# Attention row sums in a hybrid decoder layer: the diagonal pieces added on GpSimd in place of matmuls with a column of ones

## The chip, the cores and the metric

One core of one Trainium2 chip runs the whole layer in one launch. The metric is the device time in microseconds of an execution; the time before is the median of three runs. The profile shows one execution in full: TensorE matmuls (PE), its weight loads (PEld), VectorE (DVE), ScalarE (ACT), GpSimd (POOL), SyncE (SP, which issues the DMAs here) and the DMA queues.

## The reference, cut to what matters

16 learned meta tokens stand ahead of 2048 tokens (L = 2064, D = 1024). After a layer norm, one projection gives queries, keys, values, forget logits and gates for 16 heads of 64 columns, and the input of a causal pooling mixer. The attention is a causal softmax with a forget bias:

```python
s = jnp.einsum('bqhd,bkhd->bhqk', q_blk, k).astype(jnp.float32) * scale
s = s + jnp.transpose(c_blk, (0, 2, 1))[..., :, None] - c_k[:, :, None, :]
mask = key_pos[None, :] <= q_pos[:, None]
s = jnp.where(mask[None, None], s, -jnp.inf)
p = jax.nn.softmax(s, axis=-1).astype(v.dtype)
return jnp.einsum('bhqk,bkhd->bqhd', p, v)
```

Both mixers are gated, joined, projected with `w_out`, added to the scaled input and normalized again. All of it is float32. The change touches how the denominator of the softmax, the sum of `p` over the keys, is made.

## The kernel before, in words

**Stages.** The projections run first (to about 1360 us of the span), then the attention (`phase_b`, to about 2252), in which matmuls of the output projection are strewn between as filler, then the rest of the output projection and the last layer norm (`phase_c`).

**Precision.** A float32 value is kept as a high part in the matmul's own format (float32r) and a low part, the rest: `ph` and `pl` are the high and the low part of exp of the scores, `th` and `tl` those of a sum.

**Attention.** The queries of a head are cut into four blocks j = 0..3 of 512 (64 blocks for 16 heads; the first 14 heads in turn, the last two interleaved). A block works through its keys in units (`units`, line 903): units i = 0..4j are one tile of 128 keys for all 512 queries; unit 4j+1 has 400 queries left of the diagonal; the last unit, 4j+2, packs three pieces of 272, 144 and 16 queries. The piece of 16 is the corner: its keys are the 16 that 128-key tiles leave over, kept in rows 112 to 127 of `vc`. Units i < 4j lie wholly below the diagonal. There are 576 units in all.

**What a unit issues.** `emit_s` (line 959): two score matmuls per piece into the PSUM tile `s` (four buffers), a mask matmul in bf16 on the diagonal; ACT's exp into `ph`, and exp again over `s`. `emit_pl` (line 996): DVE's `pl` = `s` − `ph`, which frees the buffer of `s`. `emit_pv` (line 1015), four units later (`LAG`): the matmuls with the values. A value tile has the 64 low columns, the 64 high columns and two columns of ones, so `xo` collects `ph` times both halves, and `yo` collects `pl` times the high half, with the sum of `pl` in the rows behind it.

**The row sums of `ph`** come in two ways. For units i < 4j, POOL adds pairs of `ph` tiles (`acc` for the first pair, `tu` for others, three buffers; lines 988 to 994), DVE adds `tu` to `acc` three units later (line 1000), and behind the last of these it splits `acc` into `th` and `tl` (lines 1001 to 1006). Two matmuls with `zo`, whose first 64 columns are zero and last two are one, then add both to `yo` in the block's last unit (lines 1037 to 1039). For the units on the diagonal, each piece has a matmul of its own with `zo` (line 1036). A block with j = 0 has only these. The corner's three matmuls contract over rows 96 to 127 (lines 1030 and 1041).

When a block ends, ACT copies `yo` (`c1`), DVE adds the high and low parts into `araw`, and the sum's row goes out by DMA; every second head, `chunk_end` (line 917) brings the reciprocal back by DMA and gates: two multiplies and a subtraction on POOL, a cast on DVE.

**Order.** Instructions of PE, DVE, ACT and POOL are chained by hand in the order in which the program is written (`in_order`, line 65), so each engine's queue is that order. The loop at line 1085 writes for each unit m: its scores, then filler matmuls by a weight (two for units left of the last two, one for those), `emit_pl(m)`, `emit_pv(m - LAG)`, loads, and in every second unit a round of delayed work (`service`: gating, weight splits).

Of the kernel before, what the change touches and what calls it, by code (L numbers as in the profile page):

```python
# [9 lines left out]
F32 = mybir.dt.float32  # L10
# [25 lines left out]
def f32(ap):  # L36
    return ap.bitcast(F32)
# [3 lines left out]
def kernel(  # L41
# [78 lines left out]

    # rows of a head: c high and low, k high, k low, q low, q high, -max high and low
    kqd = dtile("kqd", [H, 260, L], F32)
# [603 lines left out]
    def kv_set(pl, s):  # L726
# [4 lines left out]
        nc.gpsimd.memset(f32(ka[0:2, :]), 1.0)  # L731
        nc.gpsimd.memset(f32(vc[96:P]), 0.0)
        for v in (vt, vc):
# [51 lines left out]
    def prefetch(n, nv):  # L785
        """Loads at most one piece of keys and values ahead of head order, and queries two steps ahead."""
        k = 0
# [171 lines left out]
    def emit_s(m):  # L959
# [27 lines left out]
        late_pl[m] = (ps, ph, pl, off)  # L987
        if i < 4 * j and i % 2:
            tag = "acc" if i == 1 else "tu"
            tu = bp.tile([P, 512], F32, tag=tag, name=tag, bufs=2 if i == 1 else 3)  # L990
            if i == 1:
                accs[n] = tu
            nc.gpsimd.tensor_tensor(out=tu, in0=f32(units_state[m - 1][0]), in1=f32(ph), op=ALU.add)
            units_tu[m] = tu

    def emit_pl(m):
        n, i, u, nu = seq[m]
        h, j = seqn[n]
        if 6 <= i and i % 2 == 0:
            nc.vector.tensor_tensor(out=accs[n], in0=accs[n], in1=units_tu.pop(m - 3), op=ALU.add)  # L1000
            if i == 4 * j + 2:
                th = bp.tile([P, 512], F32R, tag="th", name="th")
                tl = bp.tile([P, 512], F32R, tag="tl", name="tl")
                nc.vector.tensor_copy(out=th, in_=accs[n])
                nc.vector.tensor_tensor(out=tl, in0=accs[n], in1=f32(th), op=ALU.subtract)
                accs[n] = (th, tl)
        ps, ph, pl, off = late_pl.pop(m)
        nc.vector.tensor_tensor(
            out=pl[:, :off], in0=ps[:, :off], in1=f32(ph[:, :off]), op=ALU.subtract
        )  # L1010
# [4 lines left out]
    def emit_pv(m):  # L1015
# [9 lines left out]
        np_ = len(places)  # L1025
        full = i < 4 * j
        for idx, (kt, q0, w, off) in enumerate(places):
            first = i == 0 and idx == 0
            sl = slice(off, off + w)
            rows, v = (slice(96, P), vc[:, j]) if w == NM else (slice(0, P), vt[:, kt])  # L1030
            mm(
                xo[:, q0:512], v[rows, 0:P], ph[rows, sl],
                start=first, stop=last_u and idx == np_ - 1,
            )
            if not full:
                mm(yo[0 : DH + 2, q0:512], zo[rows], ph[rows, sl], start=first, stop=False)
        if last_u and j:
            for t in accs.pop(n):
                mm(yo[0 : DH + 2, :], zo, t, start=False, stop=False)
        for idx, (kt, q0, w, off) in enumerate(places):  # L1040
            rows, v = (slice(96, P), vc[:, j]) if w == NM else (slice(0, P), vt[:, kt])
            mm(
                yo[0 : DH + 2, q0:512], v[rows, DH:], pl[rows, off : off + w],
                start=full and i == 0 and idx == 0, stop=last_u and idx == np_ - 1,
            )
        if last_u:
            c1 = bp.tile([65, 512], F32, tag="c1", name="c1", bufs=2)
            nc.scalar.copy(out=c1, in_=yo[0:65, :])
# [36 lines left out]
    for m in range(nseq + LAG):  # L1085
# [11 lines left out]
        if m < nseq:  # L1097
            emit_pl(m)
        if m >= LAG:
            emit_pv(m - LAG)  # L1100
# [133 lines left out]
```

## Time and profile before

| | |
|---|---|
| Median of 3 runs | 2431.03 us (2428.52 to 2432.9) |
| Profiled execution, span from first to last instruction | 2432.5 us (mean granted clock 0.992; its device time is not listed apart from the span) |
| PE busy | 2366.8 us, 97%, 11706 matmuls |
| PEld busy | 1947.5 us, 80% |
| DVE busy | 1430.4 us, 59% |
| ACT busy | 960.6 us, 39% |
| POOL busy | 716.2 us, 29% |
| Matmuls of `ph` with `zo`, 512 wide | 64, mean 394 ns each |
| Matmuls `th` with `zo` | 48, mean 448 ns each |
| POOL pair sums `tu` / `acc` | 144 / 48, mean 1328 / 1301 ns |

A row of a group names the engine, the operation, out<-in by the program's names, the shape and the count. Matmuls record `out<-moving,stationary`, with rows*columns of the weights and then the moving tile; `128*66 128x512` is 66 columns of weights on 128 rows against 512 moving columns. Their records overlap, so the mean duration of one is longer than what it adds to the time. All instructions go through one helper, so all carry the line L86 and are told apart by their tiles.

### The profile page before, as it was taken

What the parts mean: (1) busy time and instruction counts of PE and PEld (TensorE: products, weight loads), DVE (VectorE), ACT (ScalarE), POOL (GpSimd) and SP (SyncE); (2) the same over time, 40 slices, a digit from 0 to 9 for tenths busy, and PEclk for the clock granted to TensorE, in tenths of its full rate; (3) what the DMA queues carried; (4) which work ended last, traced back from release to release, by engine and by line L of the source; (5) the groups of instructions that cost most, each with busy time, mean ns of one, the idle gap of its engine ahead of it and who ended that gap; (6) DMA issues with size and microseconds to landing.
All of it is one profiled execution on the core that took longest, in us unless ns stands there. A gap on an engine that the chain in (4) does not pass through costs nothing.

```text
span 2432.5 us, 32725 instructions
## 1 busy us (share of the span) xinstructions
PE 2366.8 (97%) x11706; PEld 1947.5 (80%) x11706; DVE 1430.4 (59%) x2116; ACT 960.6 (39%) x1813; POOL 716.2 (29%) x531
## 2 busy tenths in 40 slices
PE   6999999999999999999999899999999999999998
PEld 5778799898898988988887677777777777776787
DVE  6631145644655556545433578778778777777356
ACT  4431221211212222111111577777777777766000
POOL 4730021222223314230101134344353544444000
PEclk9999999999999999999999999999999999999999
DMA  7853222222222212222223657566566657555955
GB/s 254 262 162 92 61 85 61 96 63 78 88 62 88 81 60 88 68 92 75 75 81 111 174 159 210 153 189 181 168 187 179 199 168 215 161 164 158 286 187 164
DMA packets 317506, 333.59 MB, mean 137 GB/s; under 512 B 27744, under 2 KB 241072, under 8 KB 317312
## 3 DMA queue, kind: packets, MB, share of 16 engines
q1 hardware_dynamic: 317344, 331.51, 44.4%
q8 instruction: 92, 1.51, 0.3%
q14 instruction: 70, 0.57, 0.1%
HBM read 207.43 MB, written 124.00 MB: 136 GB/s over the span
## 4 chain that ended last, share of the span: by engine, by line
PE 91%; DVE 3%; DMA 2%; issue 1%; ACT 1%; POOL 0%; SPq 0%; DVEq 0%; ACTq 0%; POOLq 0%
PE d L86 59%; PE s L86 12%; PE yo L86 8%; PE mx L86 6%; PE xo L86 5%; DVE pl L86 1%; PE tr L86 1%; DMA xm<-xa 1%; DMA wu<-in_wut_dram 0%; SPq L86 0%; DVE acc L86 0%; DMA xt<-in_x_dram 0%; DVE s L86 0%; DMA wv<-in_wv_dram 0%; DMA kb<-kqd 0%
## 5 line engine op out<-in xcount | busy, mean ns | idle before, releaser
L86 PE MATMUL d<-hh,wh 128*128 128x412 f32 (+2 forms) x1472 | 561.4, 381 | 0.0
L86 PE MATMUL d<-hl,wh 128*128 128x412 f32 (+2 forms) x1472 | 538.6, 366 | 0.0
L86 PE MATMUL d<-hh,wl 128*128 128x412 f32 (+2 forms) x1472 | 538.4, 366 | 0.0
L86 DVE TENSOR_REDUCE mxs<-mx 128x1 f32<-128x912 f32 (+14 forms) x416 | 358.3, 865 | 279.1 <-PE mx L86 274.5
L86 DVE TENSOR_TENSOR pl<-s,ph 128x512 fp32r<-128x512 f32 (+2 forms) x576 | 376.3, 664 | 185.8 <-ACT s L86 179.6
L86 ACT ACTIVATE ph<-s 128x512 fp32r<-128x512 f32 (+2 forms) x576 | 335.0, 582 | 186.6 <-PE s L86 171.9
L86 PE MATMUL d<-wh,xm 128*128 128x512 f32 x1024 | 355.0, 403 | 4.6 <-DMA xm<-xa 3.8
L86 ACT ACTIVATE s<-s 128x512 f32<-128x512 f32 (+2 forms) x576 | 332.4, 577 | 0.0
L86 PEld LDWEIGHTS d<-hl,wh 128*128 128x128 f32 x1472 | 278.5, 189 | 23.1
L86 PEld LDWEIGHTS d<-hh,wl 128*128 128x128 f32 x1472 | 277.1, 188 | 23.4
L86 PEld LDWEIGHTS d<-hh,wh 128*128 128x128 f32 x1472 | 280.7, 191 | 18.2
L86 PE MATMUL s<-qa,ka 68*128 68x512 f32 (+4 forms) x704 | 265.2, 377 | 15.9 <-DVE pl L86 15.9
L86 POOL TENSOR_TENSOR wl<-wst,wh 128x1024 fp32r<-128x1024 f32 x40 | 96.2, 2405 | 576.4 <-ACT wh L86 576.3
L86 PE MATMUL s<-qb,kb 128*128 128x512 f32 (+4 forms) x704 | 253.0, 360 | 0.0
L86 POOL TENSOR_TENSOR tu<-ph 128x512 f32<-128x512 f32 x144 | 190.9, 1328 | 154.4 <-ACT ph L86 128.3
L86 PE MATMUL xo<-ph,vt 128*128 128x512 f32 (+3 forms) x640 | 233.0, 368 | 0.0
L86 PEld LDWEIGHTS d<-wh,xm 128*128 128x128 f32 x1024 | 193.5, 190 | 44.4 <-issue 3.3
L86 PE MATMUL yo<-pl,vt 128*66 128x512 f32 (+3 forms) x640 | 223.7, 366 | 0.9 <-ACT c L86 0.9
L86 PE MATMUL mx<-ka,qa 66*128 66x512 f32 (+5 forms) x704 | 199.4, 350 | 6.6 <-ACT qa L86 3.8
L86 PE MATMUL d<-wl,xm 128*128 128x512 f32 x512 | 205.6, 402 | 0.0
L86 PEld LDWEIGHTS s<-qa,ka 68*128 68x128 f32 x704 | 134.8, 191 | 71.6 <-DVE pl L86 27.4
L86 PEld LDWEIGHTS mx<-ka,qa 66*128 66x128 f32 x704 | 133.0, 190 | 23.8 <-ACT qa L86 5.2
(143 smaller groups left out, 3079.0 us busy)
## 6 DMA issues: line engine op xcount, KB each, us to landing
xm<-xp SPq DMA_DIRECT2D x32, 1024.0 KB
xm<-xa SPq DMA_DIRECT2D x20, 1024.0 KB
vd<-vs SPq DMA_DIRECT2D x32, 512.0 KB
vt<-vd SPq DMA_DIRECT2D x64, 256.0 KB
qb<-kqd SPq DMA_DIRECT2D x64, 256.0 KB
xa<-am SPq DMA_DIRECT2D x32, 512.0 KB
xp<-pm SPq DMA_DIRECT2D x32, 412.0 KB
kqd<-lo SPq DMA_DIRECT2D x64, 206.0 KB
```

The source lines that it names most:

```text
L86: return in_order(f(*a, **k))
```

## The change

The diagonal pieces' matmuls with `zo` go. In their place POOL adds the diagonal units into the same sums: unit 4j and unit 4j+1 into the last `tu`, DVE adds that to `acc` when the last unit's scores are issued, and POOL adds the last unit's three pieces to `acc`. A block with j = 0 starts `acc` from its first two units, with a copy for the 112 columns that the second does not have. `th` and `tl` are made for every block, two units after the last (`emit_sums`), and their matmuls come last in `yo`. The corner's matmuls contract over all 128 rows; for that `vc` is zeroed in all rows (the masked `ph` and `pl` are zero there).

```diff
@@ kv_set
-        nc.gpsimd.memset(f32(vc[96:P]), 0.0)
+        nc.gpsimd.memset(f32(vc), 0.0)
@@ emit_s
-        if i < 4 * j and i % 2:
-            tag = "acc" if i == 1 else "tu"
-            tu = bp.tile([P, 512], F32, tag=tag, name=tag, bufs=2 if i == 1 else 3)
-            if i == 1:
-                accs[n] = tu
-            nc.gpsimd.tensor_tensor(out=tu, in0=f32(units_state[m - 1][0]), in1=f32(ph), op=ALU.add)
-            units_tu[m] = tu
+        row_sums(m)
+
+    def pool_add(out, a, b):
+        nc.gpsimd.tensor_tensor(out=out, in0=a, in1=b, op=ALU.add)
+
+    def row_sums(m):
+
+        n, i, u, nu = seq[m]
+        h, j = seqn[n]
+        ph, _, places = units_state[m]
+        ph = f32(ph)
+        if i == 1:
+            accs[n] = bp.tile([P, 512], F32, tag="acc", name="acc", bufs=2)
+        if i < 4 * j:
+            if i % 2:
+                tu = accs[n]
+                if i > 1:
+                    tu = bp.tile([P, 512], F32, tag="tu", name="tu", bufs=3)
+                    units_tu[n, i] = tu
+                pool_add(tu, f32(units_state[m - 1][0]), ph)
+        elif i == 4 * j:
+            if j:
+                tu = units_tu[n, i - 1]
+                pool_add(tu, tu, ph)
+        elif i == 4 * j + 1:
+            (_, q0, w, off), = places
+            if j:
+                tu = units_tu[n, i - 2]
+                pool_add(tu[:, q0:], tu[:, q0:], ph[:, :w])
+            else:
+                first = f32(units_state[m - 1][0])
+                nc.gpsimd.tensor_copy(accs[n][:, :q0], first[:, :q0])
+                pool_add(accs[n][:, q0:], first[:, q0:], ph[:, :w])
+        else:
+            if j:
+                vec_add(n, i - 3)
+            for _, q0, w, off in places:
+                pool_add(accs[n][:, q0:], accs[n][:, q0:], ph[:, off : off + w])
+            sums_due.append((m + 2, n))
+
+    def vec_add(n, i):
+        nc.vector.tensor_tensor(out=accs[n], in0=accs[n], in1=units_tu.pop((n, i)), op=ALU.add)
+
+    sums_due = deque()
+
+    def emit_sums(m):
+        while sums_due and sums_due[0][0] <= m:
+            n = sums_due.popleft()[1]
+            th = bp.tile([P, 512], F32R, tag="th", name="th")
+            tl = bp.tile([P, 512], F32R, tag="tl", name="tl")
+            nc.vector.tensor_copy(out=th, in_=accs[n])
+            nc.vector.tensor_tensor(out=tl, in0=accs[n], in1=f32(th), op=ALU.subtract)
+            accs[n] = (th, tl)
@@ emit_pl
-        if 6 <= i and i % 2 == 0:
-            nc.vector.tensor_tensor(out=accs[n], in0=accs[n], in1=units_tu.pop(m - 3), op=ALU.add)
-            if i == 4 * j + 2:
-                th = bp.tile([P, 512], F32R, tag="th", name="th")
-                tl = bp.tile([P, 512], F32R, tag="tl", name="tl")
-                nc.vector.tensor_copy(out=th, in_=accs[n])
-                nc.vector.tensor_tensor(out=tl, in0=accs[n], in1=f32(th), op=ALU.subtract)
-                accs[n] = (th, tl)
+        if 6 <= i <= 4 * j and i % 2 == 0:
+            vec_add(n, i - 3)
@@ emit_pv
-        full = i < 4 * j
         for idx, (kt, q0, w, off) in enumerate(places):
             first = i == 0 and idx == 0
             sl = slice(off, off + w)
-            rows, v = (slice(96, P), vc[:, j]) if w == NM else (slice(0, P), vt[:, kt])
+            v = vc[:, j] if w == NM else vt[:, kt]
             mm(
-                xo[:, q0:512], v[rows, 0:P], ph[rows, sl],
+                xo[:, q0:512], v[:, 0:P], ph[:, sl],
                 start=first, stop=last_u and idx == np_ - 1,
             )
-            if not full:
-                mm(yo[0 : DH + 2, q0:512], zo[rows], ph[rows, sl], start=first, stop=False)
-        if last_u and j:
-            for t in accs.pop(n):
-                mm(yo[0 : DH + 2, :], zo, t, start=False, stop=False)
         for idx, (kt, q0, w, off) in enumerate(places):
-            rows, v = (slice(96, P), vc[:, j]) if w == NM else (slice(0, P), vt[:, kt])
+            v = vc[:, j] if w == NM else vt[:, kt]
             mm(
-                yo[0 : DH + 2, q0:512], v[rows, DH:], pl[rows, off : off + w],
-                start=full and i == 0 and idx == 0, stop=last_u and idx == np_ - 1,
+                yo[0 : DH + 2, q0:512], v[:, DH:], pl[:, off : off + w],
+                start=i == 0 and idx == 0, stop=False,
             )
         if last_u:
+            th, tl = accs.pop(n)
+            mm(yo[0 : DH + 2, :], zo, th, start=False, stop=False)
+            mm(yo[0 : DH + 2, :], zo, tl, start=False, stop=True)
             c1 = bp.tile([65, 512], F32, tag="c1", name="c1", bufs=2)
@@ loop over units
         if m < nseq:
             emit_pl(m)
+        emit_sums(m)
         if m >= LAG:
             emit_pv(m - LAG)
```

## The prediction

> **What bounds the kernel now.** I read the busy time by stage first, then the waits inside the longest stage that the diff touches, then single instructions. The stage runs from the last projection matmul to the last attention unit. Columns are the stretch, its length, busy time and instruction count of PE, PEld, DVE, ACT and POOL, the granted clock, and the DMA share and rate.
>
> ```profile
> 1360.00:2252.00 892.00, 874.90 (x4365) 661.16 (x4363) 690.79 (x1064) 651.52 (x1246) 376.52 (x286) 0.99 0.61 180
> 2252.00:2432.50 180.50, 167.88 (x720) 136.03 (x720) 94.03 (x139) 8.45 (x21) 4.26 (x3) 0.97 0.68 214
> ```
>
> The attention stage is 892 us of the span of 2432.5. PE is busy for 874.9 of them, DVE for 690.8 and POOL for 376.5. The waits of that stage say who holds PE up when something does (us in total, times, longest):
>
> ```profile
> PEld s L86 <- DVE pl L86: 27.4, 27, 3.0
> ...
> PE s L86 <- DVE pl L86: 15.9, 18, 2.6
> ```
>
> The two rows are one and the same wait seen from the weight load and from the matmul: the score matmul of a unit needs the PSUM bank that `pl`, four units earlier, has to give back. So some 27 us of the 892 are lost to DVE, and the rest is matmul after matmul. A matmul taken out shortens the stage by its slot, until DVE is late more often.
>
> **What a matmul costs here.** PE's records overlap, so a slot is the distance from one start to the next, not the duration in the second column. These rows are the last three units of one query block with j = 2:
>
> ```profile
> 1607.20 0.40 PE L86 MATMUL yo<-ph,zo 128*66 128x512 f32 x1
> 1607.43 0.39 PE L86 MATMUL yo<-pl,vt 128*66 128x512 f32 x1
> ...
> 1608.77 0.34 PE L86 MATMUL yo<-ph,zo 128*66 128x400 f32 x1
> 1608.94 0.35 PE L86 MATMUL yo<-pl,vt 128*66 128x400 f32 x1
> ...
> 1610.07 0.28 PE L86 MATMUL xo<-ph,vt 128*128 128x272 f32 x1
> 1610.19 0.29 PE L86 MATMUL yo<-ph,zo 128*66 128x272 f32 x1
> 1610.31 0.23 PE L86 MATMUL xo<-ph,vt 128*128 128x144 f32 x1
> 1610.38 0.23 PE L86 MATMUL yo<-ph,zo 128*66 128x144 f32 x1
> 1610.54 0.27 PE L86 MATMUL xo<-ph,vc 32*128 32x16 f32 x1
> 1610.67 0.20 PE L86 MATMUL yo<-ph,zo 32*66 32x16 f32 x1
> 1610.80 0.45 PE L86 MATMUL yo<-th,zo 128*66 128x512 f32 x1
> 1611.09 0.39 PE L86 MATMUL yo<-tl,zo 128*66 128x512 f32 x1
> 1611.32 0.35 PE L86 MATMUL yo<-pl,vt 128*66 128x272 f32 x2
> 1611.60 0.22 PE L86 MATMUL yo<-pl,vc 32*66 32x16 f32 x1
> 1611.75 0.50 PE L86 MATMUL s<-qa,ka 68*128 68x512 f32 x1
> 1612.09 0.40 PE L86 MATMUL s<-qb,kb 128*128 128x512 f32 x1
> ```
>
> The 512-wide matmul with the ones column has a slot of 0.23 us, the 400-wide one 0.17. The last unit, from its first matmul (1610.07) to the second score matmul behind it (1612.09), takes 2.02. In it every step into or out of the corner's 32 rows is long: 0.16 from the 144-wide matmul into the corner where the other 144-wide slot is 0.07; 0.13 and 0.13 inside; 0.29 for `th` and 0.34 for the next score matmul where a 512-wide one has 0.23. The next fence gives a 16-wide matmul on more rows, and the two ends of the last unit of a block with j = 0, which has no `th` and `tl` (1.56 us from 1636.74 to 1638.30):
>
> ```profile
> 1629.08 0.26 PE L86 MATMUL s<-qa,ka 68*128 68x16 f32 x1
> 1629.19 0.26 PE L86 MATMUL s<-qb,kb 128*128 128x16 f32 x1
> ...
> 1636.74 0.28 PE L86 MATMUL xo<-ph,vt 128*128 128x272 f32 x1
> ...
> 1638.30 0.39 PE L86 MATMUL s<-qb,kb 128*128 128x512 f32 x1
> ```
>
> A 16-wide score matmul, the next load being 128 columns wide, has a slot of 0.11. So sixteen columns are not what makes the corner slow; the change to 32 rows and back is the nearer reading. I take the long slots as gone once the corner uses all rows, and bound that from the other side below. The Trainium skill, page TensorEngine Tiling (Array Packing), section Key Properties, says that changing the tiling mode drains TensorE: by that rule the extra 0.09 to 0.11 at each switch goes with the 32 rows (67.5 us in the sum below), without it the gain would be 40. The trace agrees with the rule as far as it goes, since no corner on 128 rows has been run.
>
> **The change, part by part.** *Removed on PE.* Five matmuls with the ones column in each of the 64 query blocks. The new last unit I build from slots above: 272-wide 0.12; 144-wide before a 128-column load 0.11; corner 0.07 (there is no such row: it lies between 0.04 and the 0.13 of the old corner, and 0.07 is that of 144 columns before a 66-column load); 272-wide 0.12; 144-wide 0.07; corner 0.07; `th` 0.23; `tl` 0.23; first score matmul 0.23. That is 1.25 against 2.02, so 0.77 less. With 0.23 and 0.17 from the two units before, a block with j > 0 loses 1.17 us; 48 blocks give 56.
>
> *Added on PE.* The 16 blocks with j = 0 now need `th` and `tl` as well, which the 1.25 contains: 1.56 − 1.25 = 0.31, with 0.23 and 0.17 it is 0.71 each, 11.4 together. PE's account is 56 + 11.4 = 67.5 us less. If the corner kept its long slots on 128 rows (0.16, 0.13, 0.16, 0.13, then 0.29 and 0.34), the unit would take 1.68: 0.43 less saved in 64 units, 27.5, and a gain of 40. That is the lower bound of this term.
>
> *Added on POOL.* Each block gets an add of 512, one of 400, and 272, 144 and 16; with j = 0 a copy of 112 takes the place of the 512.
>
> ```profile
> L86 DVE TENSOR_TENSOR acc<-acc,tu x144: 643/790/1780, 1372.5 to 2237.7; 128x512 f32<-128x512 f32 x144
> L86 POOL TENSOR_TENSOR acc<-ph x48: 1269/1295/1442, 1366.3 to 2223.3; 128x512 f32<-128x512 f32 x48
> L86 DVE CAST th<-acc x48: 426/427/1412, 1373.2 to 2239.1; 128x512 fp32r<-128x512 f32 x48
> L86 DVE TENSOR_TENSOR tl<-acc,th x48: 691/693/1734, 1373.7 to 2239.5; 128x512 fp32r<-128x512 f32 x48
> ```
>
> ```profile
> L86 POOL TENSOR_TENSOR pm<-s,pm 128x400 fp32r<-128x400 f32 x8 | 8.8, 1097 | 18.6 <-ACT pm L86 18.6
> ```
>
> 512 columns take 1.30 us and 400 take 1.10. The narrow ones have no row; they lie between nothing and the 1.10 of 400 columns, and the line through the two rows puts 272, 144, 112 and 16 at 0.87, 0.64, 0.59 and 0.42 (an estimate). So 4.33 us in 48 blocks and 3.62 in 16: 266 us on POOL, which then is busy 643 of about 835. That is below PE's 874.9 − 67.5 = 807, so as an average it stays hidden behind the matmuls.
>
> *Added and moved on DVE.* `th` and `tl` for 16 more blocks: 16 × (0.43 + 0.69) = 18 us. The sums into `acc` stay at 144 in number. In each block with j > 0 the last of them is now issued with the scores of the last unit and waits for POOL's 400-wide add of the unit before. Behind it in DVE's queue stand the `pl` of the last unit and a filler's `yt`; the score matmul four units on waits for that `pl`. `th` and `tl` move two units later, behind two more `pl`, and out from in front of the last unit's `pl`, which helps exactly the wait above. In exchange PE reaches them with two units of cover where it had four. POOL's adds also hold `ph` longer, for ACT's exp six units later; six units of 892 / 576 = 1.55 us on average cover that, and if POOL fell further behind, ACT would wait.
>
> *The corner's memset* covers 128 rows in place of 32:
>
> ```profile
> L86 POOL MEMSET vc<- x4: 113/321/527, 1313.0 to 1359.9; 32x520 f32 x2, 128x8 f32 x2
> ```
>
> Two instructions of at most 0.53 us, before the stage and beside projection matmuls; uncovered, and even at twice the time, the two cost 1.1 us more. I take nothing. Dropping a comment and a docstring costs nothing.
>
> **What DVE's crowding gives back.** Where heads meet, the last block of one (j = 3) and the first of the next (j = 0) are six short units in a row:
>
> ```profile
> 1675.00:1691.00 16.00, 15.09 (x82) 11.17 (x82) 12.70 (x20) 9.86 (x20) 7.68 (x7) 1.00 0.66 190
> ```
>
> ```profile
> 1684.50 0.50 PE L86 MATMUL s<-qa,ka 68*128 68x512 f32 x1 [0.91 <-DVE pl L86]
> ```
>
> DVE works 12.70 of 16 us here and PE already waits 0.91. Afterwards PE needs 15.09 − 1.17 − 0.71 = 13.2 and DVE 12.70 + 1.12 = 13.8: in this stretch DVE becomes the longer one, by 0.6, besides the wait it already causes. With POOL's later sums I count about 0.75 us for each of 16 such places, where nothing happens at best and 1.9 (all that was saved there) at worst: 12 us, between 0 and 30.
>
> The sum: 2432.5 − 67.5 + 12 = 2377 for the profiled execution. Its span is 1.5 above the median of the runs, 2431.0, and inside their spread, and no other time of that execution is shown, so I take 1.5 off: **2375.5, say 2375 us**.
>
> **The rivals.** *DVE gets locked out.* Two rows of the same moment, POOL first:
>
> ```profile
> 1604.63 1.63 POOL L86 TENSOR_TENSOR araw<-araw,sg 128x512 f32<-128x512 f32 x1
> ```
>
> ```profile
> 1605.14 1.41 DVE L86 CAST th<-acc 128x512 fp32r<-128x512 f32 x1
> ```
>
> The cast takes 0.43 by the median and 1.41 here, and is over as POOL's multiply is (1606.26, and 1606.55). The `acc` sums spread from 643 to 1780 ns in the same way. With POOL busy for 643 us in place of 376, `th` meets it more often, and half of the extra 0.98, 0.5 us, on PE's path at 64 block ends is 32 us. Then 2375 + 32 = 2407. For it: the cover is down to two units. Against: `pl` reads PSUM, is 376 of DVE's 691 busy us, and shows no such spread. The Trainium skill, page SBUF — State Buffer, section Who interferes with whom, calls the port pair of the two engines an exclusive lock on which the loser blocks for the whole instruction; the trace agrees (1.41 against 0.43), and by that rule alone this rival, with its 2407, would be the forecast.
>
> *Slower.* POOL's in-order queue makes the new chain late, and PE waits at every block end for the last sum, `th` and `tl`. If one 512-wide POOL instruction (1.30) stands uncovered in front of each, 64 × 1.30 = 83 us are lost against 67.5 won: 2431 + 16 = 2447. It decides from 67.5 / 64 = 1.05 us per block. For it: the gating multiplies of 1.3 to 1.6 us sit in the same queue. Against: they come for one head pair at a time, so for at most half the blocks, and two units last 3.1 us on average.
>
> *The corner stays slow* (40 in place of 67.5): 2375 + 27.5 = 2403.
>
> *More than the slots.* With `th` and `tl` out from in front of `pl`, the present waits go too, half of the 27.4 or so, and nothing is given back: 2375 − 12 − 14 = 2349.
>
> *The change does nothing measurable*: losses meet the gain, 2431.
>
> **How the numbers follow.** Forecast 0.64, locked out 0.15, corner slow 0.06, more than the slots 0.08, nothing 0.03, slower 0.04. The range 2356 to 2406 leaves out the half of the locked-out case that lies above, half of the larger gain, and the last two: about 0.19. All but the last two are faster by over 0.2% (4.9 us, about what a measurement of this kernel can tell from no change): 0.93, 0.03 and 0.04.
>
> **What would show it.** Right: no group of the ones column with `ph`; a last unit of 1.25 us; POOL up by some 266 us; a stage of about 835 us with PE near 97% busy. Wrong: corner slots still near 0.13 to 0.16; PE's waits in front of `th` or `tl`, ended by DVE, of more than 12 us together; DVE's `acc` waiting for POOL by tens of us; or ACT's exp waiting for POOL.

## The result and the profile after

The changed kernel takes 2452.03 us, the median of four runs (2449.76 to 2452.72), against 2430.08 us for the kernel before in the same comparison: a ratio of 1.008, 95% interval 1.0066 to 1.0094. It is slower by about 22 us where the forecast was faster by 56, and it lies outside the range of 2356 to 2406. The profiled execution took 2449.76 us, with a span of 2448.1 and a mean granted clock of 0.979 (0.992 before).

First the attention stage in the table of stretches of the changed kernel, with the columns of the prediction's first fence:

```profile
1360.00:2252.00 892.00, 832.96 (x4037) 629.61 (x4036) 739.28 (x1089) 646.57 (x1240) 627.33 (x602) 0.96 0.60 178
```

In the same 892 us PE is busy for 42 us less, DVE for 48 more and POOL for 251 more, and the granted clock is 0.96 where it was 0.99. Work has left PE, and the stage is not shorter for it. From first to last matmul of the attention (first score matmul to last `yo`) it went from 886.6 to 895.5 us, and what follows from 186.7 to 193.5. The page's engine rows and its chain of waits say the same of the whole execution:

```profile
PE 2335.2 (95%) x11418; PEld 1924.0 (79%) x11418; DVE 1484.5 (61%) x2148; ACT 958.2 (39%) x1813; POOL 969.2 (40%) x851
...
PE 78%; DVE 6%; POOL 6%; DMA 4%; issue 3%; ACT 2%; SPq 1%; POOLq 0%; ACTq 0%; DVEq 0%
```

Before, the chain that ended last was PE for nearly all of the span:

```profile
PE 91%; DVE 3%; DMA 2%; issue 1%; ACT 1%; POOL 0%; SPq 0%; DVEq 0%; ACTq 0%; POOLq 0%
```

Now DVE and POOL carry 6% each. There are 288 matmuls fewer (11418 for 11706: five less in each of 64 blocks, two more in 16 of them). What PE now waits for stands in the waits of the attention stage (us in total, times, longest):

```profile
DVE acc L86 <- POOL tu L86: 41.4, 48, 3.0
PEld yo L86 <- DVE tl L86: 36.5, 37, 1.7
...
PEld s L86 <- DVE pl L86: 30.4, 34, 3.5
...
PEld yo L86 <- DVE th L86: 19.7, 22, 2.0
```

The waits for `th` and `tl` have no row before. By the weight loads they are 36.5 + 19.7 = 56.2 us in 59 waits. By the starts of the matmuls these lie at 36 of the 64 block ends, 23 of which have both. The old wait, for `pl`, is still there (30.4; 27.4 before). And DVE waits for POOL's `tu` 48 times. By the starts 41 of these waits, 33 of the 41.4 us, lie in front of the last sum of one of the 48 blocks with j > 0, behind the 400-wide add; the other 7 are as in the kernel before, whose row is

```profile
DVE acc L86 <- POOL tu L86: 8.0, 7, 1.3
```

One junction of heads shows how it goes (the timeline of the changed kernel, engines mixed; start, duration, instruction, and in brackets its idle time before and what ended it):

```profile
1904.09 0.51 ACT L86 ACTIVATE ph<-s 128x400 fp32r<-128x400 f32 x1 [0.34 <-PE s L86]
...
1904.14 1.28 POOL L86 TENSOR_TENSOR am<-araw,am 128x512 fp32r<-128x512 f32 x1 [0.36 <-DVE am L86]
...
1905.38 1.05 POOL L86 TENSOR_TENSOR tu<-tu,ph 128x400 f32<-128x400 f32 x1
...
1906.46 0.69 DVE L86 TENSOR_TENSOR acc<-acc,tu 128x512 f32<-128x512 f32 x1 [1.92 <-POOL tu L86]
...
1907.30 1.63 POOL L86 TENSOR_TENSOR acc<-acc,ph 128x272 f32<-128x272 f32 x3 [0.87 <-DVE acc L86]
...
1907.73 0.50 PE L86 MATMUL s<-qa,ka 68*128 68x512 f32 x1 [1.32 <-DVE pl L86]
...
1908.96 0.47 DVE L86 CAST th<-acc 128x512 fp32r<-128x512 f32 x1 [0.21 <-POOL acc L86]
...
1909.46 1.40 DVE L86 TENSOR_TENSOR tl<-acc,th 128x512 fp32r<-128x512 f32 x1
1909.48 0.45 PE L86 MATMUL yo<-th,zo 128*66 128x512 f32 x1
...
1910.92 0.45 PE L86 MATMUL yo<-tl,zo 128*66 128x512 f32 x1 [0.99 <-DVE tl L86]
...
1913.86 1.30 POOL L86 TENSOR_TENSOR araw<-araw,rb 128x512 f32<-128x512 f32 x1
...
1914.07 1.38 DVE L86 CAST th<-acc 128x512 fp32r<-128x512 f32 x1
...
1914.63 0.35 PE L86 MATMUL xo<-ph,vt 128*128 128x272 f32 x2
...
1914.82 0.22 PE L86 MATMUL xo<-ph,vc 128*128 128x16 f32 x1
...
1914.89 0.39 PE L86 MATMUL yo<-pl,vt 128*66 128x272 f32 x2
...
1915.12 0.17 PE L86 MATMUL yo<-pl,vc 128*66 128x16 f32 x1
...
1915.24 1.33 POOL L86 TENSOR_TENSOR araw<-araw,sg 128x512 f32<-128x512 f32 x1
...
1915.55 1.57 DVE L86 TENSOR_TENSOR tl<-acc,th 128x512 fp32r<-128x512 f32 x1
...
1917.18 0.45 PE L86 MATMUL yo<-tl,zo 128*66 128x512 f32 x1 [1.22 <-DVE tl L86]
```

In the first block, behind ACT's exp and a gating multiply on POOL, there is one chain that goes back and forth between engines: POOL's 400-wide add, DVE's sum, POOL's three pieces, DVE's `th` and `tl`, PE. From 1905.38 to 1910.92 it has hardly a gap, and PE stands at its end. In the second block (from 1913.86) the two engines take turns: `th` starts inside POOL's first multiply and ends at 1915.45, 0.29 after it; POOL's next multiply starts at 1915.24, `tl` starts inside it, takes 1.57 and ends 0.55 after it. Unhindered they take 0.43 and 0.69.

The second block is nearer to the rule than the first. Only at 14 of the 64 block ends does `th` start within 0.1 us of the end of POOL's last piece. At the other 50 that piece was done over 0.3 us before, and `th` came from its place in DVE's queue, behind `pl` of the second unit after the block.

### The profile page after: what moved, and what is told of

Same layout as the page of the kernel before. It is cut to its first block, busy times and chain, and to the rows that moved or that the text cites. A ratio compares the mean times of both kernels' runs of the same rounds, so it can differ in the third digit from the quotient of the medians.

```text
span 2448.1 us, 32638 instructions
## 1 busy us (share of the span) xinstructions
PE 2335.2 (95%) x11418; PEld 1924.0 (79%) x11418; DVE 1484.5 (61%) x2148; ACT 958.2 (39%) x1813; POOL 969.2 (40%) x851
## 4 chain that ended last, share of the span: by engine, by line
PE 78%; DVE 6%; POOL 6%; DMA 4%; issue 3%; ACT 2%; SPq 1%; POOLq 0%; ACTq 0%; DVEq 0%
PE d L86 56%; PE s L86 8%; PE mx L86 6%; PE yo L86 4%; PE xo L86 3%; POOL tu L86 2%; DVE tl L86 2%; POOL araw L86 1%; POOL acc L86 1%; DVE th L86 1%; ACT ph L86 1%; DVE pl L86 1%; DMA rb<-rd 1%; DMA rd<-st 1%; PE tr L86 1%
## 5 line engine op out<-in xcount | busy, mean ns | idle before, releaser
L86 PE MATMUL s<-qb,kb 128*128 128x512 f32 (+4 forms) x704 | 258.3, 368 | 0.0
L86 PE MATMUL yo<-pl,vt 128*66 128x512 f32 (+3 forms) x640 | 229.7, 375 | 0.0
L86 PEld LDWEIGHTS s<-qa,ka 68*128 68x128 f32 x704 | 138.5, 197 | 74.5 <-DVE pl L86 30.4
L86 DVE TENSOR_TENSOR acc<-acc,tu 128x512 f32<-128x512 f32 x144 | 135.7, 943 | 41.5 <-POOL tu L86 41.4
```

The lines of the kernel that those rows point to most:

```text
L86: return in_order(f(*a, **k))
```

## The experiments

All times are medians of device time; each ratio is to the kernel before on the same chip, whose medians were 2429.3 to 2432.2. The table is worked out from the starts of all matmuls of the attention stage in each trace: the distance from one start to the next counts as work up to the tenth percentile of that pair of instructions in that kernel (in front of `th` up to 0.03, of `tl` up to 0.23), and what is over that counts as lost in front of the later one. Losses under 0.26 at a halved clock stand in a column of their own, and smaller kinds are left out (29 to 42 us in each kernel).

| kernel | stage | PE's work | lost before `th`, `tl` | lost before the first score matmul | lost to halved clock | clock halved for | behind the stage |
|---|---|---|---|---|---|---|---|
| before | 886.6 | 821 | 3 | 20 | 4 | 10 | 186.7 |
| changed | 895.5 | 761 | 55 | 24 | 26 | 68 | 193.5 |
| e1: corner alone | 856.4 | 793 | 2 | 22 | 3 | 7 | 186.5 |
| e2: PE doesn't wait for `th`, `tl` | 864.0 | 762 | 0 | 46 | 14 | 34 | 194.1 |
| e3: four units of cover | 858.7 | 761 | 9 | 36 | 13 | 31 | 185.9 |
| e8: e3, cover two again | 894.9 | 761 | 45 | 31 | 24 | 61 | 181.5 |
| e12: `th` on ACT | 868.4 | 761 | 31 | 27 | 16 | 44 | 193.5 |
| e14: e2, no `th`, `tl` | 829.2 | 762 | 0 | 26 | 4 | 10 | 188.9 |
| e5: e1 and POOL's load | 883.2 | 793 | 2 | 36 | 14 | 38 | 186.8 |
| e4: POOL adds two units | 851.2 | 774 | 12 | 20 | 7 | 20 | 184.2 |

The theory after the result: the prediction's account of PE's work was right, and PE now waits for a sum that comes late through POOL and DVE, with too little cover, that is, too little work of PE between the issue of `th` and `tl` and the matmuls that read them (theory A). The rivals: POOL's load by itself hinders DVE, whoever reads the sums (B); the corner on 128 rows saved nothing (C).

### The corner alone (e1_corner)

From the kernel before, with the second edit in the matmuls of `xo` and of `yo`:

```diff
-        nc.gpsimd.memset(f32(vc[96:P]), 0.0)
+        nc.gpsimd.memset(f32(vc), 0.0)
-            rows, v = (slice(96, P), vc[:, j]) if w == NM else (slice(0, P), vt[:, kt])
+            rows, v = slice(0, P), vc[:, j] if w == NM else vt[:, kt]
```

> The kernel before, with the corner's three matmuls on all 128 rows and the memset that this needs, and nothing else of the change. If the long slots round the corner belong to the 32 rows, each of the 64 last units gets about 0.43 us shorter on PE: 2430 - 27 = about 2403 us. If they belong to the 16 columns, or if DVE is late there anyway, the time stays within 2425 to 2431.

Measured: 2402.3 us, ratio 0.9878 [0.9863, 0.9893]. One block's end, with all its ones matmuls still there (timeline, PE):

```profile
1568.07 0.29 PE L86 MATMUL xo<-ph,vt 128*128 128x272 f32 x1
...
1568.38 0.23 PE L86 MATMUL yo<-ph,zo 128*66 128x144 f32 x1
1568.45 0.22 PE L86 MATMUL xo<-ph,vc 128*128 128x16 f32 x1
1568.52 0.20 PE L86 MATMUL yo<-ph,zo 128*66 128x16 f32 x1
1568.58 0.43 PE L86 MATMUL yo<-th,zo 128*66 128x512 f32 x1
...
1569.28 0.17 PE L86 MATMUL yo<-pl,vc 128*66 128x16 f32 x1
1569.31 0.47 PE L86 MATMUL s<-qa,ka 68*128 68x512 f32 x1
1569.62 0.39 PE L86 MATMUL s<-qb,kb 128*128 128x512 f32 x1
```

The corner's slots are 0.07, 0.06 and 0.03 where they were 0.13, 0.13 and 0.15, and from the first matmul to the second score matmul the unit takes 1.55 in place of 2.02. C falls: these three lines of the change bring 30 us.

### Does PE wait for th and tl, and what does cover do? (e2_free, e3_lag6, e8_lag6_late)

e2, from the changed kernel, in which the matmuls at a block's end read a constant tile, so that the output lacks the sums of `ph`:

```diff
+    tz = kvs[0].tile([P, 512], F32R, tag="tz", name="tz")
+    nc.vector.memset(f32(tz), 1.0)
-            th, tl = accs.pop(n)
-            mm(yo[0 : DH + 2, :], zo, th, start=False, stop=False)
-            mm(yo[0 : DH + 2, :], zo, tl, start=False, stop=True)
+            accs.pop(n)
+            mm(yo[0 : DH + 2, :], zo, tz, start=False, stop=False)
+            mm(yo[0 : DH + 2, :], zo, tz, start=False, stop=True)
```

e3, from the changed kernel, also with LAG + 1 buffers of `pl` and one each of `c1` and `t`:

```diff
-    LAG = 4
+    LAG = 6
```

e8, from e3:

```diff
-            sums_due.append((m + 2, n))
+            sums_due.append((m + 4, n))
```

> The changed kernel, in which the two matmuls at a block's end read a constant tile in place of th and tl (all adds, th and tl are still made on GpSimd and VectorE; the output lacks the sums of ph). Cover theory (PE loses its gain by waiting for th and tl, some 55 us, and by the halved clock that these pauses bring, some 22 us): about 2375 to 2385 us, no half-speed stretches beyond those of before. Load theory (VectorE and GpSimd as a whole are behind, whoever waits): the waits come back in front of the score matmuls, which wait for pl, and the time stays at 2430 or above.

> The changed kernel with the value matmuls six units behind the scores in place of four (ph gets eight buffers, pl seven, c1 and t one each). th and tl then have four units of cover in place of two. Cover theory: nearly all of the wait for th and tl goes, 2380 to 2395 us. Load theory: 2430 us or above, the waits now in front of the score matmuls.

> The changed kernel with six units between scores and values (2405), but th and tl made four units after the last, not two, so that they have two units of cover again. Cover theory: the waits for th and tl come back, 2435 to 2455 us. If the further buffers and the longer lag themselves made the 47 us: it stays at 2405 to 2415.

Measured: without the wait 2416.78 us, ratio 0.994 [0.9923, 0.9957], between the two ranges that were expected; with four units of cover 2404.98, 0.9886 [0.9868, 0.9905], 10 above the expected range; with the longer lag and the cover of two again 2435.61, 1.0019 [1.001, 1.0028]. PE's waits in front of `yo` with four units of cover:

```profile
PEld yo L86 <- DVE tl L86: 8.3, 8, 1.5
```

and with the same lag and two units:

```profile
PEld yo L86 <- DVE tl L86: 40.5, 40, 1.6
```

e3 and e8 differ in nothing but where `th` and `tl` are issued, and 31 us lie between them: the two units are what PE misses, not the lag. e8's stage is as long as that of the changed kernel (894.9 for 895.5); its shorter time lies mostly behind the stage (181.5 for 193.5). A is shown, for 31 us by e8 and 35 by e2. But with both waits gone e2's stage is still 102 us longer than PE's work in it, where that of the corner alone is 63 longer: A is not all.

### What remains when PE does not wait? (e12_act_th, e13_free_late_vec, e14_free_no_split)

e12, from the changed kernel:

```diff
-            nc.vector.tensor_copy(out=th, in_=accs[n])
+            nc.scalar.copy(out=th, in_=accs[n])
```

e13, from e2 (like e14 without the sums of `ph` in its output), with the last sum and POOL's three pieces issued behind the last unit's `pl`:

```diff
-            if j:
-                vec_add(n, i - 3)
-            for _, q0, w, off in places:
-                pool_add(accs[n][:, q0:], accs[n][:, q0:], ph[:, off : off + w])
+            last_sum.append((n, i, j, ph, places))
...
     def emit_sums(m):
+        if last_sum:
+            n, i, j, ph, places = last_sum.pop()
+            if j:
+                vec_add(n, i - 3)
+            for _, q0, w, off in places:
+                pool_add(accs[n][:, q0:], accs[n][:, q0:], ph[:, off : off + w])
```

e14, from e2:

```diff
-            th = bp.tile([P, 512], F32R, tag="th", name="th")
-            tl = bp.tile([P, 512], F32R, tag="tl", name="tl")
-            nc.vector.tensor_copy(out=th, in_=accs[n])
-            nc.vector.tensor_tensor(out=tl, in0=accs[n], in1=f32(th), op=ALU.subtract)
-            accs[n] = (th, tl)
```

> The changed kernel with the copy into th on ScalarE in place of VectorE. Lock theory: th is no longer blocked by GpSimd (21 us in the changed kernel) and VectorE has 49 us less to do: 2425 to 2440. If only the late sum from GpSimd matters, th waits for it on ScalarE as well, exps stand behind it, and the time stays at 2450 or rises.

> As e2 (the block-end matmuls read a constant tile, the output lacks the sums of ph; 2417), with VectorE's last sum of a block and GpSimd's three pieces issued behind pl of the last unit in place of ahead of it. If it is this sum, waiting for GpSimd (36 us in e2) with pl queued behind it, that keeps e2 46 us above the 2371 that its matmuls would give, 2395 to 2408. If it is VectorE's blocked time, which the order does not change, 2412 to 2420.

> As e2, with th and tl not made at all (GpSimd's adds and VectorE's acc sums stay; the output lacks the sums of ph). If VectorE's load with th and tl and their blocked time (123 us in e2) is what remains, 2375 to 2390. If the wait of the last sum for GpSimd is, 2405 to 2417.

Measured: `th` on ACT 2422.59, ratio 0.997 [0.9959, 0.9982]; the last sum behind `pl` 2417.15, 0.9949 [0.9931, 0.9966]; no `th` and `tl` 2379.89, 0.9791 [0.9768, 0.9814]. On ACT the cast takes 603 to 627 ns at all 64 block ends, so POOL's adds do not lengthen it there. Moving the last sum behind `pl` wins nothing (e13 as e2): DVE's wait for POOL in front of the sums falls from 36.5 to 19.2 us, but `th` and `tl` take 23 us more. In e14 that wait is still there (48.6), and the stage is 67 us longer than PE's work in it, about as with the corner alone (63), so it costs little. The split itself, `th` and `tl` on DVE, is what was left: without it the same POOL adds run and 37 us go. In e2 PE's wait for `pl` had grown:

```profile
PEld s L86 <- DVE pl L86: 64.5, 69, 4.0
```

and without the split it is near the old one:

```profile
PEld s L86 <- DVE pl L86: 36.4, 39, 4.0
```

The split delays the `pl` behind it. In e2 it takes 122.9 us on DVE, where 64 unhindered pairs would take 64 × 1.12 = 72; e14 removes both parts, the work and the hindrance. The groups of the attention stage for the kernel before (busy us, mean ns of one, and the idle time before them):

```profile
L86 DVE TENSOR_TENSOR tl<-acc,th 128x512 fp32r<-128x512 f32 x48 | 36.2, 754 | 1.6
L86 DVE CAST th<-acc 128x512 fp32r<-128x512 f32 x48 | 23.4, 488 | 1.7
```

and the changed kernel:

```profile
L86 DVE TENSOR_TENSOR tl<-acc,th 128x512 fp32r<-128x512 f32 x64 | 69.5, 1085 | 3.1
...
L86 DVE CAST th<-acc 128x512 fp32r<-128x512 f32 x64 | 48.7, 760 | 8.8 <-POOL acc L86 8.7
```

Against the unhindered 427 and 693 ns the blocked time is 64 × (0.333 + 0.392) = 46.4 us, where it was 48 × (0.061 + 0.061) = 5.9. Those 40 us more, and 18 for the split of 16 more blocks, are the 58.6 us by which `th` and `tl` together take longer than before; all of DVE's work in the 892 us is 48 more.

### Is it POOL's load, whoever reads the sums? (e5_load, e9_load_const, e10_load_memset)

e5, from e1, with the change's adds on POOL into a tile that nobody reads:

```diff
+    def load(q0, w, src):
+        nc.gpsimd.tensor_tensor(out=sc[:, q0 : q0 + w], in0=sc[:, q0 : q0 + w], in1=src, op=ALU.add)
...
+        if i == 4 * j and j:
+            load(0, 512, f32(ph))
+        elif i == 4 * j + 1:
+            if not j:
+                nc.gpsimd.tensor_copy(sc[:, 0:112], f32(units_state[m - 1][0])[:, 0:112])
+            load(112, 400, f32(ph)[:, 0:400])
+        elif i == 4 * j + 2:
+            for _, q0, w, o in places:
+                load(q0, w, f32(ph)[:, o : o + w])
```

e9, from e5, with the scratch tile added to itself, so that `ph` is not held (and no copy):

```diff
-        nc.gpsimd.tensor_tensor(out=sc[:, q0 : q0 + w], in0=sc[:, q0 : q0 + w], in1=src, op=ALU.add)
+        nc.gpsimd.tensor_tensor(out=sc[:, q0 : q0 + w], in0=sc[:, q0 : q0 + w], in1=sc[:, q0 : q0 + w], op=ALU.add)
```

e10, from e9, with about as much POOL time in memsets (POOL is busy for 600 us from 1360 to 2200, 581 in e9 and 371 with the corner alone):

```diff
-        nc.gpsimd.tensor_tensor(out=sc[:, q0 : q0 + w], in0=sc[:, q0 : q0 + w], in1=sc[:, q0 : q0 + w], op=ALU.add)
+        left = {512: 1280, 400: 1024, 272: 752, 144: 464, 16: 176}[w]
+        while left:
+            nc.gpsimd.memset(sc[:, 0 : min(left, 512)], 0.0)
+            left -= min(left, 512)
```

> The kernel with the corner alone on 128 rows (2402), and beside it the same extra adds on GpSimd as in the change, into a scratch tile that nobody reads. VectorE's and TensorE's instructions and their waits are those of the corner alone. Load theory (GpSimd's mere presence locks VectorE out of its sums, th and tl, so pl comes late): 2415 to 2425 us. Cover theory (only the waits that the change adds, of PE for th and tl and of DVE for GpSimd's sum, cost anything): within 4 us of 2402.

> The corner alone (2402) with the same GpSimd adds as e5 (2429), but adding the scratch tile to itself: they read no ph, so they hold no buffer and wait for nothing. If the 26 us of e5 come from GpSimd's reads shutting VectorE out (54 us more of blocked th, tl and acc there), 2418 to 2430. If they come from ph being kept longer (ACT waited 12 us for GpSimd in e5), 2402 to 2412.

> As e9, but GpSimd is kept busy for about the same time by memsets, which write and read nothing. If it is GpSimd's reading that blocks VectorE's two-input sums (acc, tl), the blocked time falls back to about that of the corner alone, 55 us, and the time to 2402 to 2410. If any GpSimd instruction blocks them, as long as e9.

Measured: e5 2428.79, ratio 0.999 [0.998, 0.9999]; e9 2421.92, 0.9963 [0.995, 0.9975]; e10 2407.17, 0.9904 [0.9891, 0.9918]. Against the corner alone (2402.3) adds that nobody reads cost 26 us, adds that don't touch `ph` 20, and memsets of about the same time 5. The instructions of `acc`'s users in e9 (duration ns: shortest, median, longest):

```profile
L86 DVE CAST th<-acc x48: 426/748/1419, 1372.0 to 2228.6; 128x512 fp32r<-128x512 f32 x48
L86 DVE TENSOR_TENSOR tl<-acc,th x48: 691/798/1693, 1372.5 to 2230.1; 128x512 fp32r<-128x512 f32 x48
```

and in e10:

```profile
L86 DVE CAST th<-acc x48: 426/620/1867, 1372.9 to 2211.4; 128x512 fp32r<-128x512 f32 x48
L86 DVE TENSOR_TENSOR tl<-acc,th x48: 691/693/1677, 1373.7 to 2213.3; 128x512 fp32r<-128x512 f32 x48
```

With adds on POOL both are mostly hindered; with memsets `tl` is at its 693 by the median and only the cast still is not (427 with the corner alone). By the mean the cast takes 590 ns with the corner alone, 742 beside the memsets and 835 beside the adds of e9, the subtraction 774, 835 and 934. The Trainium skill, page SBUF — State Buffer, section Who interferes with whom, says that a VectorE instruction with two SBUF inputs meets the lock only against a GpSimd operation that reads SBUF, and one in a two-port mode, which it says a copy or cast can enter, against any. Both pairs of medians agree; by the means the memsets are not wholly without effect on the subtraction, and why is open.

The load does not act by making POOL's own sums late: DVE's wait for `tu` is 7.9 us in e5, e9 and e10 and 8.1 with the corner alone. It acts through `pl`, which stands behind the blocked instructions. PE's wait for it is 28.7 us with the corner alone, in e9

```profile
PEld s L86 <- DVE pl L86: 37.9, 33, 2.8
```

and in e10

```profile
PEld s L86 <- DVE pl L86: 29.4, 29, 2.2
```

B holds beside A: the load alone, off every path of data to PE, takes back 20 to 26 of the 30 us that the corner had won. The 7 between e5 and e9 have two possible causes that no run separates. `th`, `tl` and the sums into `acc` take 24 us more on DVE in e5. And `ph` is held longer, as the prediction names: in e5 ACT's exp waits for POOL's adds for 12.0 us (5.2 in e9), where it did not with the corner alone:

```profile
ACT ph L86 <- POOL sc L86: 12.0, 7, 3.7
```

### Other ways to make the sums (e4_two_units, e7_two_lag6, e11_two_lag5, e6_fp32)

e4, from the changed kernel: the last unit, and blocks with j = 0, keep the ones matmuls; the last sum, `th` and `tl` follow the last unit's `pl`, four units ahead of their matmuls:

```diff
-            if j:
-                vec_add(n, i - 3)
-            for _, q0, w, off in places:
-                pool_add(accs[n][:, q0:], accs[n][:, q0:], ph[:, off : off + w])
-            sums_due.append((m + 2, n))
+        elif j:
+            sums_due.append((m, n))
...
             n = sums_due.popleft()[1]
+            vec_add(n, 4 * seqn[n][1] - 1)
...
+            if last_u or not j:
+                mm(yo[0 : DH + 2, q0:512], zo, ph[:, sl], start=first, stop=False)
```

e7, from e4 (LAG + 1 buffers of `pl`, one each of `c1` and `t`); e11 is the same with 5 and two each of `c1` and `t`:

```diff
-    LAG = 4
+    LAG = 6
```

e6, from the changed kernel, with `th` and `tl` not made:

```diff
-            mm(yo[0 : DH + 2, :], zo, th, start=False, stop=False)
-            mm(yo[0 : DH + 2, :], zo, tl, start=False, stop=True)
+            mm(yo[0 : DH + 2, :], f32(zo), accs.pop(n), start=False, stop=True)
```

> The corner on 128 rows; GpSimd adds only units 4j and 4j+1 of the blocks with j > 0 (2.4 us each in 48 blocks); the last unit's three pieces and the blocks with j = 0 keep their matmuls with the ones column. The last sum, th and tl follow pl of the last unit at once, with four units of cover. PE has 27 + 48 x 0.40 = 46 us less to do than before. Cover theory: 2384 to 2392 us. Load theory (115 us more on GpSimd cost DVE its time): 2403 or above, no better than the corner alone.

> Units 4j and 4j+1 on GpSimd and the corner on 128 rows (2394), with six units between scores and values in place of four. Its waits for th and tl (12 us with the halved clock behind them) should go: 2380 to 2388 us by the cover theory; 2392 to 2396 if DVE's load sets what is left.

> Units 4j and 4j+1 on GpSimd and the corner on 128 rows (2394), with five units between scores and values and c1 and t at two buffers as before (six units with one buffer each came out at 2405). Its 12 us of waits for th and tl should shrink: 2384 to 2392 if the single buffers were what six units lost by; 2396 or above if the longer lag itself costs.

> The changed kernel without th and tl: one matmul in full float32 adds acc to yo. VectorE loses 64 casts and 64 subtractions (118 us with their blocked time), PE waits for GpSimd's last piece alone; the float32 matmul should cost about 0.4 us more than the two that it replaces, 25 us in all. Lock theory (VectorE's share of the chain, th 0.76 and tl 1.09 us on average, is what PE waits for): the wait at the block ends shrinks to under 15 us in total, the time is 2390 to 2405. If GpSimd's own chain is what is late, PE waits as long as before for acc: 2440 or above.

Measured: e4 2394.33, ratio 0.9845 [0.983, 0.986], the fastest of those with the whole output; with lag 6 (e7) 2405.14, 0.9888 [0.9872, 0.9905], slower than either theory expected; with lag 5 (e11) 2399.79, 0.9875 [0.986, 0.9891]; one full float32 matmul (e6) 2402.75, 0.9881 [0.9865, 0.9896]. In e4 the 48 blocks with j > 0 leave only the two wide adds to POOL, nothing narrow stands between the last sum and `th`, and its weight loads wait for

```profile
PEld yo L86 <- DVE tl L86: 6.9, 9, 1.7
PEld yo L86 <- DVE th L86: 4.0, 6, 2.4
```

10.9 us in place of 56.2. Beside the corner alone that is worth 8 us more: PE's work is 19 less, and about 14 of it goes in waits and clock. Lag 6 lengthens its stage (863.6 for 851.2; lost before the first score matmul 36 for 20), lag 5 does not (848.7) and is longer behind the stage (189.5 for 184.2); the reason is open. In e6 the float32 matmul replaces `th` and `tl` on DVE and two matmuls:

```profile
1619.18 1.05 PE L86 MATMUL yo<-acc,zo 128*66 128x512 f32 x2
1619.67 0.80 PE L86 MATMUL s<-qa,ka 68*128 68x512 f32 x1
1620.30 0.40 PE L86 MATMUL s<-qb,kb 128*128 128x512 f32 x1
```

It shows as two records with 0.49 us together, as much as the two matmuls it replaces, but the slot of the score matmul behind it is 0.63 where 0.23 is usual. From 1619.18 to 1620.30 are 1.12, so the float32 matmul costs 0.89, about four slots of 0.23; the 0.4 at 64 block ends is 26 us and leaves e6 level with the corner alone. The Trainium skill, page FP8 and Floating Point Precision, section TensorE Precision Notes, gives true float32 four passes, and the trace agrees.

In e6 PE reads POOL's sum itself, and with the split off DVE it hardly waits for it:

```profile
PEld yo L86 <- POOL acc L86: 1.1, 2, 0.7
```

So POOL's pieces alone do not come late for PE: the time is in the range of the lock theory, and far from the 2440 or above that was expected if GpSimd's own chain were late. What came late in the changed kernel was mostly the split behind them, on DVE.

## Why the prediction was wrong

**What PE was to lose: right.** Predicted 67.5 us, measured 821 − 761, about 60. The last unit of the second block of the timeline needs 0.49 from 1914.63 to 1915.12, and the slots that the prediction built (0.12, 0.11, 0.07, 0.12, 0.07) make 0.49. The corner on 128 rows has 0.07 as assumed. The extra at each switch of rows was put at 27.5 in 64 units, and e1 measured 30. That agrees with the rule of the Trainium skill, page TensorEngine Tiling (Array Packing), section Key Properties, that a change of the tiling mode drains TensorE.

**POOL: right in size, wrong as harmless.** 251 us more for 266: the 400-wide add took 1.05 and the three narrow ones together 1.63 at the junction shown, for 1.10 and 1.93. The conclusion "as an average it stays hidden behind the matmuls" compared busy times, and e5 and e9 show that the load costs 20 to 26 us though PE reads none of it.

**The step that failed** is the term "What DVE's crowding gives back": 12 us, between 0 and 30. It was priced by the busy time of DVE in the 16 junctions. Measured, the stage gave back about 69 us (60 less work, yet 8.9 longer): 52 more in front of `th` and `tl`, 22 more by the halved clock, 4 more in front of the score matmuls, and 9 less in smaller kinds. The stage is not short of DVE time on average (739 of 892 us). The prediction wrote the step down, "In exchange PE reaches them with two units of cover where it had four", and gave it no price of its own.

What two units have to cover is `th` and `tl` from their place in DVE's queue, as long as they take beside POOL's adds. The trace of the changed kernel, gone through block end by block end, gives the price. At the 12 ends where neither is blocked (`th` under 0.5, `tl` under 0.8 us) PE loses 0.4 us in all; at the 18 where both are, 32 of the 55. With the unhindered 0.43 and 0.69 from the same starts about 18 of the 55 would be left (an estimate from the trace, end by end).

The 14 ends where `th` follows POOL's last piece at once hold 20 of the 55, and there the chain was too long from the start. The prediction's own durations had it: 1.10 for the 400-wide add, 0.64 for the sum, 0.87 + 0.64 + 0.42 on POOL, 0.43 and 0.69 make 4.79 us one after the other on two engines. At the first end of the junction shown, one of the 14, the second last unit's exp ends at 1904.60 (1904.09 + 0.51), and `tl`'s matmul could have followed `th`'s at 1909.71 (1909.48 + 0.23): 5.11 us, of which PE stood 1.32 for `pl`. Without that wait 3.8 us are left for a chain of 4.79, before anything hinders it; and there POOL's add began 0.8 late, behind the gating multiply, and `tl` took 1.40 for 0.69.

**"DVE gets locked out", 2407 at 0.15: right in kind, too small.** It took half of one extra 0.98 per block end, 32 us. The blocked time of `th` and `tl` is 46.4 us, 0.73 per block end. And it meets a cover that suffices only for unblocked durations: e12 takes only the cast off DVE and wins 29, e14 takes the split away and wins 37 from e2. Its reason against, that `pl` reads PSUM and shows no spread, is true of `pl` and beside the point, since `pl` waits in the queue behind a blocked `tl`.

**"Slower", 2447 at 0.04: nearest to the time.** The place is right (59 waits for `th` or `tl`, though at 36 of the 64 block ends), and it needed more than 1.05 us per block: 69 / 64 = 1.08 in the stage. That its time came so near is in part luck: its price was one POOL instruction uncovered at every end, and the trace shows `th` and `tl` blocked on DVE at many ends, POOL's pieces late at 14, and the halved clock. Its reason against, "two units last 3.1 us on average", took the average of all units, and the two behind a block's end were not timed.

**"The corner stays slow"** fell with e1; **"more than the slots"** too: the wait for `pl` did not go (30.4 us for 27.4). `pl` is not held up by `th` and `tl` alone: without them, in e14, it is still 36.4.

**ACT's exp** waits for POOL's sums in `acc` for 4.8 us and in `tu` for 2.8 in the changed kernel, so that the longer hold on `ph` costs little. The 6.8 us behind the stage were not foreseen: after 2230 us PE's wait for the last gated rows, `xm` by DMA, is 9.9 us for 3.8. POOL's gating of the last block stands behind the new adds there; that is read from the trace, and no run takes it apart.

What is shown, then, is two costs that overlap: cover (e2, e3, e8) and the hindrance of DVE by POOL (e5, e9 and e10; e6, e12 and e14 take the split off DVE, its work and its hindrance together). They are not to be added, because a blocked `tl` counts in both.

## What to carry to other kernels

When work moves from the engine that bounds a kernel to idle ones, a sum of busy times does not show that it stays hidden: write the new chain down instruction by instruction, across engines, each at its place in its engine's queue and with the longest durations that the trace shows beside the medians, and set it against the time the bounding engine needs from the same start to the point where it reads the result, at the place where that is shortest. On VectorE and GpSimd count each other's instructions as hindrance, since adds that nobody read cost 20 to 26 us here where the matmuls that they replace are 32 (793 less 761). And split a change with several parts before judging it: three lines of this one, the corner, were worth 30 us, and the version that left the narrow adds on PE 38.

## What the runs showed of the hardware

- GpSimd adds into a scratch tile cost 20 to 26 us of 2402, memsets of about the same busy time 5 (e9, e5, e10): that GpSimd reads matters, not only how long it runs.
- Narrow adds on GpSimd are dear for their width: a 16-wide one takes a quarter of a 512-wide one in e9 (groups, mean ns before the last bar), and 0.23 us in the changed kernel:

```profile
L86 POOL TENSOR_TENSOR sc<-sc 128x512 f32<-128x512 f32 x48 | 63.9, 1331 | 0.0
...
L86 POOL TENSOR_TENSOR sc<-sc 128x16 f32<-128x16 f32 x64 | 21.8, 341 | 5.0
```

- With waits of at most 2.0 us in front of `th` and `tl` the clock was at half for 68 us of the stage, against 10 before and 10 in e14; over the kernels of the table the halved time rises roughly with the time lost in waits. The Trainium skill, page TensorE: Matmul & The Clock Gate, Part 1, puts the fall to half clock after an idle window of about 3.4 us, and tells of a kernel whose frequent short idles between groups of matmuls made the clock go up and down. These pauses are shorter than the window one by one, so the trace agrees with the second. How many have to come together, no run here takes apart.
- A full float32 matmul, 512 wide, costs 0.89 us where one in float32r costs 0.23, and half of it shows only as a longer slot of the next matmul (e6).
